# A gated expansion of tokens: the gates move to GpSimd's queue, the first two tokens to the head of SyncE's

## The chip, the cores and the metric

The kernel runs on one core of a Trainium2 chip. The metric is the device time of one execution in microseconds (us); lower is better. Before the change the median of three runs is 92.47 us (92.43 to 92.58). The profile is a separate look at one execution; its span, from the first to the last instruction of the program, is 90.7 us.

## The reference

Each of 8 x 256 = 2048 tokens has a row `x` of 512 values and 8 gate weights. The gates of a token are divided by their sum, and the output holds the token's row eight times, once scaled by each gate:

```python
x:            (8, 256, 512) float32
gate_weights: (8, 256, 8)   float32

gate_weights = gate_weights / (np.sum(gate_weights, axis=-1, keepdims=True) + 1e-8)
output = x[:, :, None, :] * gate_weights[:, :, :, None]      # (8, 256, 8, 512)
```

The input is 4.26 MB and the output 33.55 MB. There is one multiplication for each output value.

## The kernel before

The 2048 tokens are laid over 128 partitions, so that each partition has J = 16 neighbouring tokens. In the text, "token j" is the j-th of each partition: 128 rows of `x`. Everything is kept in SBUF: all gates, all of `x`, and a ring of 10 slots, each with room for one token's eight scaled rows.

The loads are four. The gates (64 KB) and the **head**, tokens 0 and 1 of `x` (512 KB), are moved ahead of the barrier with which the program begins; the **body**, tokens 2 to 12 (2816 KB), and the **tail**, tokens 13 to 15 (768 KB), follow after it on SyncE's queue.

```python
SLOTS = 10
HEAD = 2
TAIL = 13
CHUNKS = ((0, 2, 0), (2, 3, 2), (5, 3, 5), (8, 4, 0), (12, 4, 6))   # first token, tokens, first slot

    first_loads = [
        nc.sync.dma_start(out=g_all, in_=g_v),                                    # L68
        nc.scalar.dma_start(out=x_all[:, 0:HEAD, :], in_=x_v[:, 0:HEAD, :]),      # L69
    ]
    issue_before_entry_barrier(nc, first_loads)
    body_load = nc.sync.dma_start(                                                # L72
        out=x_all[:, HEAD:TAIL, :], in_=x_v[:, HEAD:TAIL, :]
    )
    nc.sync.dma_start(out=x_all[:, TAIL:J, :], in_=x_v[:, TAIL:J, :])             # L75
```

Here `issue_before_entry_barrier` takes the instructions out of their block and puts them at the front of the entry block, ahead of the barrier at which all engines meet.

Then come a small table load on ScalarE (`warm`), the four steps that normalize the gates on VectorE, and the scaling. For tokens 0 and 1 each of the eight experts is an instruction of its own, three on ScalarE and five on VectorE; other tokens are done whole by VectorE or by eight instructions of ScalarE.

```python
    nc.vector.reduce_sum(out=gsum, in_=g_all, axis=mybir.AxisListType.X)          # L80
    nc.vector.tensor_scalar_add(out=gsum, in0=gsum, scalar1=1e-8)                 # L81
    nc.vector.reciprocal(out=gsum, in_=gsum)                                      # L82
    nc.vector.tensor_tensor(out=gn, in0=g_all,                                    # L83
                            in1=gsum.to_broadcast([P, J, E]), op=mult)
    # ... (scale_one: L90 on ScalarE, L92 on VectorE; scale_token: L95 on VectorE)
    for j0, m, s0 in CHUNKS:
        # ... the m tokens of the chunk into slots s0 ...
        store = nc.sync.dma_start(                                                # L120
            out=out_v[:, j0 : j0 + m, :, :], in_=ring[:, s0 : s0 + m, :, :]
        )
        if j0 == 0:
            tc.add_manual_dep(store.ins, body_load.ins.name, ...,
                              reason="no store among the loads")
```

The last lines make the first store (4096 KB) wait for the landing of the body, beside the two tokens that it stores. The other stores are 6144, 6144, 8192 and 8192 KB; all five go through SyncE's queue.

Of the kernel before, what the change touches and what calls it, by code (L numbers as in the profile page):

```python
# [1 line left out]

# [4 lines left out]
# [4 lines that stand above are left out]
CHUNKS = ((0, 2, 0), (2, 3, 2), (5, 3, 5), (8, 4, 0), (12, 4, 6))  # L11


def issue_before_entry_barrier(nc, loads):
    names = [bi.ins.name for bi in loads]

    def move(nc):
        blocks = nc.main_func.blocks
        entry = blocks[0].instructions
        moved = []  # L20
        for block in blocks[1:]:
            for ins in list(block.instructions):
                if ins.name in names:
                    block.instructions.remove(ins)
                    moved.append(ins)
        assert sorted(i.name for i in moved) == sorted(names)
        for ins in moved:
            at = next(k for k, other in enumerate(entry) if other.engine == ins.engine)
            entry.insert(at, ins)

    nc.at_finalize(move)


@with_exitstack
def kernel(
    ctx: ExitStack,
    tc: tile.TileContext,
    x: bass.AP,
    gate_weights: bass.AP,
    out: bass.AP,  # L40
):
    nc = tc.nc
    P = 128

    B, S, D = x.shape
    E = gate_weights.shape[-1]
    J = B * S // P

    fp32 = mybir.dt.float32
    mult = mybir.AluOpType.mult  # L50

    x_v = x.flatten_outer_dims().rearrange("(p j) d -> p j d", p=P)
    g_v = gate_weights.flatten_outer_dims().rearrange("(p j) e -> p j e", p=P)
    out_v = out.rearrange("b s e d -> (b s) e d").rearrange(
        "(p j) e d -> p j e d", p=P
    )

    pool = ctx.enter_context(tc.tile_pool(name="pool", bufs=1))

    g_all = pool.tile([P, J, E], fp32)  # L60
    x_all = pool.tile([P, J, D], fp32)
    ring = pool.tile([P, SLOTS, E, D], fp32)
    gsum = pool.tile([P, J, 1], fp32)
    gn = pool.tile([P, J, E], fp32)
    warm = pool.tile([P, 1], fp32)

    first_loads = [
        nc.sync.dma_start(out=g_all, in_=g_v),  # L68
        nc.scalar.dma_start(out=x_all[:, 0:HEAD, :], in_=x_v[:, 0:HEAD, :]),  # L69
    ]  # L70
    issue_before_entry_barrier(nc, first_loads)
    body_load = nc.sync.dma_start(  # L72
        out=x_all[:, HEAD:TAIL, :], in_=x_v[:, HEAD:TAIL, :]
    )
    nc.sync.dma_start(out=x_all[:, TAIL:J, :], in_=x_v[:, TAIL:J, :])  # L75

    nc.vector.memset(warm, 0.0)  # L77
    nc.scalar.copy(out=warm, in_=warm)  # L78
# [4 lines that stand above are left out]
    nc.vector.tensor_tensor(  # L83
        out=gn, in0=g_all, in1=gsum.to_broadcast([P, J, E]), op=mult
    )

    def scale_one(engine, j, e, slot):
        o_ap, s_ap = ring[:, slot, e, :], gn[:, j, e : e + 1]
        if engine is nc.scalar:
            nc.scalar.mul(out=o_ap, in_=x_all[:, j, :], mul=s_ap)  # L90
        else:
            nc.vector.tensor_scalar_mul(out=o_ap, in0=x_all[:, j, :], scalar1=s_ap)  # L92

    def scale_token(j, slot):
        nc.vector.tensor_tensor(  # L95
            out=ring[:, slot, :, :],
            in0=x_all[:, j : j + 1, :].to_broadcast([P, E, D]),
            in1=gn[:, j, :].unsqueeze(2).to_broadcast([P, E, D]),
            op=mult,
        )  # L100

    for j0, m, s0 in CHUNKS:
        for i in range(m):
            j, slot = j0 + i, s0 + i
            if j < 2:
                for e in range(E):
                    on_act = e < 3
                    scale_one(nc.scalar if on_act else nc.vector, j, e, slot)
            elif j == 2:
                for e in range(E):  # L110
                    scale_one(nc.scalar, j, e, slot)
            elif j == 3:
                for e in range(E):
                    scale_one(nc.scalar if e < 2 else nc.vector, j, e, slot)
            elif i == 0:
                for e in range(E):
                    scale_one(nc.scalar, j, e, slot)
            else:
                scale_token(j, slot)
# [4 lines that stand above are left out]
            tc.add_manual_dep(  # L124
                store.ins,
                body_load.ins.name,
                mybir.DependencyInfo(
                    mybir.DependencyClass.Sync, mybir.DependencyReason.DATA
                ),
                reason="no store among the loads",  # L130
            )


# [1 line left out]
_INS = ['x', 'gate_weights']  # L135
_OUTS = [((8, 256, 8, 512), 'float32')]


# [23 lines left out]
```

## Time and profile before

| | |
|---|---|
| time, median of 3 | 92.47 us |
| span of the profile | 90.7 us |
| VectorE busy | 46.7 us |
| ScalarE busy | 26.4 us |
| bytes read, written | 4.26 MB, 33.55 MB |
| first store issued | 10.60 us |
| chunk of the first store computed | 7.96 us |

Each number of a time is counted from the first instruction of the span. A line of the profile names the line of the kernel (L68), the engine (DVE is VectorE, ACT is ScalarE, POOL is GpSimd, SP is SyncE; with a q it is the engine's sequencer, which issues transfers), the operation, output and inputs by the program's names, and how many instructions are meant. "Idle before, releaser" is the time for which the engine stood idle ahead of it, and what ended that. The list of DMA issues has the time from the issue to the landing, that is to the moment from which the waiting engines may go on. In the row of 40 slices a digit is the busy share of a fortieth of the span in tenths; transfers in long packets are counted at the slice of the packet's start or end, so neighbouring windows can swing above and below what was moved.

### The profile page before, as it was taken

To read this page: it belongs to the slowest core of one execution; us is meant where nothing else is said; L and a number is where in the kernel's file an instruction comes from. 1 tells how busy PE (TensorE), PEld (TensorE's weight loads), DVE (VectorE), ACT (ScalarE), POOL (GpSimd) and SP (SyncE) were. 2 spreads that over 40 slices of the span, in tenths; PEclk is the share of its full clock that TensorE was granted. 3 is DMA by queue.
4 is the path that set the end of the run, shared out by engine and by line. 5 is a ranking of instruction groups with operands and counts; after the bars stand their busy time and mean duration, and the time that the engine had idled before them with its cause. 6 is when DMAs were issued, how large, how long until landed. Compare 5 with 4: busy or idle time off the path is not lost.

```text
span 90.7 us, 140 instructions
## 1 busy us (share of the span) xinstructions
DVE 46.7 (52%) x30; ACT 26.4 (29%) x42; POOL 0.2 (0%) x4
## 2 busy tenths in 40 slices
DVE  0795399999999999999990495000000000000000
ACT  5393399997990000000000497000000000000000
POOL 0000000000000000000000000000000000000000
DMA  4998999999898889888988999999999982999990
GB/s 110 468 467 378 383 536 463 463 390 419 347 694 347 347 347 694 347 347 347 694 347 347 463 463 463 463 463 463 463 463 463 463 347 116 463 463 463 463 463 0
DMA packets 1296, 37.81 MB, mean 417 GB/s; under 512 B 144, under 2 KB 272, under 8 KB 528
## 3 DMA queue, kind: packets, MB, share of 16 engines
q1 hardware_dynamic: 1152, 37.29, 95.5%
q10 hardware_dynamic: 144, 0.52, 1.6%
HBM read 4.26 MB, written 33.55 MB: 417 GB/s over the span
## 4 chain that ended last, share of the span: by engine, by line
DMA 38%; DVE 17%; ACT 5%; ACTq 1%; issue 0%; SPq 0%
DMA out_dram<-ring 28%; DVE ring L95 14%; DMA x_all<-in_x_dram 11%; ACT ring L90 5%; DVE ring L92 3%; ACTq L157 1%; ACTq L90 0%; SPq L120 0%
## 5 line engine op out<-in xcount | busy, mean ns | idle before, releaser
L95 DVE TENSOR_TENSOR ring<-x_all,gn 128x4096 f32<-128x4096 f32 x9 | 39.2, 4420 | 3.5 <-DMA out_dram<-ring 3.5
L90 ACT ACTIVATE ring<-x_all,gn 128x512 f32<-128x512 f32 x40 | 24.9, 708 | 28.8 <-DMA out_dram<-ring 24.5
L92 DVE TENSOR_SCALAR ring<-x_all,gn 128x512 f32<-128x512 f32 x16 | 6.5, 482 | 2.8 <-DMA x_all<-in_x_dram 2.8
L78 ACT ACT_TABLE_LOAD x1 | 1.3, 1283 | 0.9 <-PEq L146 0.9
L80 DVE TENSOR_REDUCE gsum<-g_all 128x16 f32<-128x128 f32 x1 | 0.3, 286 | 1.6 <-DMA g_all<-in_gate_weights_dram 1.6
L77 DVE MEMSET warm<- 128x1 f32 x1 | 0.1, 59 | 1.0 <-PEq L146 1.0
L83 DVE TENSOR_TENSOR gn<-g_all,gsum 128x128 f32<-128x128 f32 x1 | 0.3, 291 | 0.0
L82 DVE RECIPROCAL gsum<-gsum 128x16 f32<-128x16 f32 x1 | 0.3, 252 | 0.0
L78 ACT COPY warm<-warm 128x1 f32<-128x1 f32 x1 | 0.2, 191 | 0.0
L81 DVE TENSOR_SCALAR gsum<-gsum 128x16 f32<-128x16 f32 x1 | 0.2, 176 | 0.0
L146 POOL MEMSET const-bfloat16-1.0<- 128x1 bf16 x1 | 0.1, 102 | 0.0
L146 POOL MEMSET const-uint8-127<- 128x1 uint8 x1 | 0.1, 102 | 0.0
L146 POOL MEMSET const-float32-0.0<- 128x1 f32 x1 | 0.1, 99 | 0.2 <-issue 0.2
L146 POOL MEMSET const-float32-1.0<- 128x1 f32 x1 | 0.1, 99 | 0.0
## 6 DMA issues: line engine op xcount, KB each, us to landing
out_dram<-ring SPq DMA_DIRECT2D x2, 6144.0 KB, 22.1
out_dram<-ring SPq DMA_DIRECT2D x1, 4096.0 KB, 11.5
x_all<-in_x_dram SPq DMA_DIRECT2D x1, 2816.0 KB, 9.6
x_all<-in_x_dram SPq DMA_DIRECT2D x1, 768.0 KB, 11.1
x_all<-in_x_dram ACTq DMA_DIRECT2D x1, 512.0 KB, 3.7
g_all<-in_gate_weights_dram SPq DMA_DIRECT2D x1, 64.0 KB, 2.6
out_dram<-ring SPq DMA_DIRECT2D x2, 28.1
```

The lines of the kernel that those rows point to most:

```text
L77: nc.vector.memset(warm, 0.0)
L78: nc.scalar.copy(out=warm, in_=warm)
L80: nc.vector.reduce_sum(out=gsum, in_=g_all, axis=mybir.AxisListType.X)
L81: nc.vector.tensor_scalar_add(out=gsum, in0=gsum, scalar1=1e-8)
L82: nc.vector.reciprocal(out=gsum, in_=gsum)
L83: nc.vector.tensor_tensor(out=gn, in0=g_all, in1=gsum.to_broadcast([P, J, E]), op=mult)
L90: nc.scalar.mul(out=o_ap, in_=x_all[:, j, :], mul=s_ap)
L92: nc.vector.tensor_scalar_mul(out=o_ap, in0=x_all[:, j, :], scalar1=s_ap)
L95: nc.vector.tensor_tensor(out=ring[:, slot, :, :], in0=x_all[:, j : j + 1, :].to_broadcast([P, E, D]), in1=gn[:, j, :].unsqueeze(2).to_bro ...
L146: nc = _bacc.Bacc("TRN2", target_bir_lowering=False, num_devices=1)
L157: with _tile.TileContext(nc) as tc:
```

## The change

The head of `x` takes the place of the gates at the front of SyncE's queue, still ahead of the barrier. The gates are loaded through GpSimd's queue, after the barrier. ScalarE issues no load any more. The purpose is to let the larger transfer start first and to spread the issuing over queues.

```diff
     first_loads = [
-        nc.sync.dma_start(out=g_all, in_=g_v),
-        nc.scalar.dma_start(out=x_all[:, 0:HEAD, :], in_=x_v[:, 0:HEAD, :]),
+        nc.sync.dma_start(out=x_all[:, 0:HEAD, :], in_=x_v[:, 0:HEAD, :]),
     ]
     issue_before_entry_barrier(nc, first_loads)
+    nc.gpsimd.dma_start(out=g_all, in_=g_v)
     body_load = nc.sync.dma_start(
         out=x_all[:, HEAD:TAIL, :], in_=x_v[:, HEAD:TAIL, :]
     )
```

The order of instructions on VectorE and ScalarE, apart from the issue that ScalarE loses, stays what it was.

## The prediction

> **What bounds the kernel now.** I read the page first, then the chain of waits, then the timeline of the first 11 us, because the change touches only the loads. On the page, the transfers are busy nearly all the time and no engine is:
>
> ```profile
> span 90.7 us, 140 instructions
> DVE 46.7 (52%) x30; ACT 26.4 (29%) x42; POOL 0.2 (0%) x4
> DMA  4998999999898889888988999999999982999990
> HBM read 4.26 MB, written 33.55 MB: 417 GB/s over the span
> ```
>
> The two compute engines are busy for 52% and 29% of the span, while the DMA row stands at 8 or 9 tenths from the second slice almost to the end. So the kernel is a stream of 37.8 MB (4.26 read, 33.55 written), and it ends when the stream ends. A change of the loads can count in two ways: it moves the start of the stream, or it tears a hole into it. The place where a hole can open is the seam between the last load and the first store. The timeline, cut to its first 11 us, shows the seam; the columns are start, length, engine, line and operation, and the bracket is the idle time before it and what ended that.
>
> ```profile
> 0.00 0.38 SPq L68 DMA_DIRECT2D g_all<-in_gate_weights_dram  x1
> 0.12 0.36 ACTq L69 DMA_DIRECT2D x_all<-in_x_dram  x1
> ...
> 0.91 0.33 SPq L72 DMA_DIRECT2D x_all<-in_x_dram  x1
> 1.30 0.42 SPq L75 DMA_DIRECT2D x_all<-in_x_dram  x1
> 2.61 0.29 DVE L80 TENSOR_REDUCE gsum<-g_all 128x16 f32<-128x128 f32 x1 [1.57 <-DMA g_all<-in_gate_weights_dram]
> ...
> 3.91 4.05 DVE L92 TENSOR_SCALAR ring<-x_all,gn 128x512 f32<-128x512 f32 x10 [0.19 <-DMA x_all<-in_x_dram]
> 10.53 11.14 ACT L90 ACTIVATE ring<-x_all,gn 128x512 f32<-128x512 f32 x18 [2.86 <-DMA x_all<-in_x_dram]
> ```
>
> The gates are on chip at 2.61, four small VectorE steps normalize them, and the first two tokens are computed from 3.91 to 7.96 (3.91 + 4.05) on VectorE; ScalarE's share ends a little earlier. Then both engines sit idle until the eleven tokens of the body land at 10.5. The SyncE queue's own waits name the same event for the first store:
>
> ```profile
> SPq L157 <- DMA out_dram<-ring: 33.1, 1, 33.1
> SPq L120 <- DMA x_all<-in_x_dram: 8.8, 1, 8.8
> ```
>
> It waits 8.8 us for the body load, and issues the store at 10.60. The first line is the end: after the last issue the queue waits 33.1 us for stores. The chunk was finished at 7.96, so the gates have **a slack of 10.51 − 7.96 = 2.55 us**: landing up to about 5.2 us they would cost nothing. The list of DMA issues gives the sizes and the time from issue to landing:
>
> ```profile
> x_all<-in_x_dram SPq DMA_DIRECT2D x1, 2816.0 KB, 9.6
> x_all<-in_x_dram SPq DMA_DIRECT2D x1, 768.0 KB, 11.1
> x_all<-in_x_dram ACTq DMA_DIRECT2D x1, 512.0 KB, 3.7
> g_all<-in_gate_weights_dram SPq DMA_DIRECT2D x1, 64.0 KB, 2.6
> ```
>
> Landings are therefore: gates 2.6, head 0.12 + 3.7 = 3.8, body 0.91 + 9.6 = 10.5, tail 1.30 + 11.1 = 12.4. The tail keeps the transfers busy while the first store gets under way. From 12.4 on there are only stores, and 33.55 MB from 12.4 to the last landing near 89.6 is 434 GB/s.
>
> One more thing is to be read from these landings, and my prediction hangs on it. The body was issued at 0.91 and the head, on another queue, was still coming in until 3.8. If the two had shared the DMA engines packet by packet, the body would have had a good part of its bytes by then. Yet from 3.8 to 10.5 it took 6.7 us for 2.88 MB, which is 430 GB/s, the full rate. So **practically all of the body came after the head**: a transfer that arrives later, on another queue, stood behind what the DMA engines had already taken up.
>
> **What the Trainium skill says.** "DMA: Bandwidth & Descriptors", section "Queues, rings and completion order": each DMA engine goes round between the queues at the granularity of packets, and drains a whole packet, typically 9 to 17 descriptors, before it switches. A load over 128 partitions is 8 rows and a completion per engine, so a packet of nine could be an engine's whole share of a load. The landings of head and body agree with that, although they don't prove it. The same page, section "SWDGE vs HWDGE vs iDMA", says that GpSimd's descriptors are made by software and put in a ring, with packets of preferably 4096 B at most; under "Specifications" it gives about 1 us to the first byte on this path against about 0.6 us for the SyncE and ScalarE queues. Here a view by windows shows no traffic before 1.0 us for the issue at 0.0, so 1.0 us is what the trace has for SyncE; no load of GpSimd is in this trace.
>
> **The change part by part.**
>
> (a) The head goes to SyncE ahead of the barrier and ScalarE's issue of 0.36 us disappears. The head starts at 0.0 instead of 0.12 and has no 64 KB of gates ahead of it (65.5 KB / 430 GB/s = 0.15 us). It lands some 0.3 us earlier, at about 3.5. Nobody gains directly: the head is used only once the gates are normalized.
>
> (b) The body and the tail are issued where they were, at about 0.9 and 1.3. The body loses the 64 KB ahead of it and lands 0.1 to 0.3 us earlier, near 10.3. The number of bytes is the same, so the stream as a whole gains nothing but a slightly fuller first microsecond: 0.2 us at most.
>
> (c) The gates leave SyncE at 0.0 and are issued by GpSimd after the barrier at about 0.9, with a slower start. I put their descriptors with the DMA engines at 0.9 + 1.0 + 0.4 to 1.0 = 2.3 to 2.9 us (1.0 measured on SyncE, 0.4 from the difference of the two figures of the skill, the rest allowance; an estimate). By then the body, ready at 0.9 + 1.0 = 1.9, is already queued on each of the 16 engines. The gates need every one of them, for 128 rows of 512 B lie on all.
>
> (d) From the landing of the gates to the end of the first chunk: 7.96 − 2.61 = 5.35, of which 0.19 was a wait for the head that is now over, so 5.2 us. If the body is drained first, the gates land with it, 10.3 + 0.15 for their own bytes = 10.5. The first chunk is then done at 10.5 + 5.2 = 15.7, and the store goes out there and not at 10.60: **5.1 us later**. The tail covers the transfers until 12.4; then they stand idle. In the old kernel the first store also stood behind the tail (11.5 us to land 4.19 MB, of which 9.7 are bytes at 434 GB/s); without it the store would land in about 11.1, which returns 0.3 us. Net +4.8 us. Later compute has 3.3 us and more in hand (the fourth store is issued at 47.76 and its predecessor lands at 51.1) and is moved along with the stores, so nothing of it is regained: 92.47 + 4.8 = **97.3 us**.
>
> **The rivals.** *The gates slip in.* If the engines switch after one row of 22.5 KB (2816 KB over 128 rows is 22.5 KB each, eight rows per engine; one row at 430/16 = 27 GB/s per engine is 0.83 us) and the eight gate rows of an engine, 4096 B, count as one packet, the gates wait for one or two body rows: 2.6 + 0.8 to 1.7 + 0.2 for the bytes + 0.4 to complete = 4.0 to 4.9. That is within the slack of 2.55 us; the first store still waits for the body and only (b) is left: 92.2 to 92.6 us. For it speaks that GpSimd's queue is one of its own; against it that the body didn't slip in beside the head. *One gate row per body row*: eight turns of 0.83 us, landing at about 2.6 + 6.7 + 0.4 = 9.7, and a time of 96.5, hardly to be told from my main case. *The gates land behind the tail as well*, at about 12.4: chunk done at 17.6, store 7.0 later, some 99 us. For it speaks that the tail is issued at 1.3, perhaps before the gate descriptors are complete. *An engine becomes the bound*: no, both compute engines have tens of microseconds to spare.
>
> **Range and chances.** The outcome has two heaps, not one. Behind the body (or one row for one) I give 0.55, slipping in 0.37, behind the tail too 0.08. Two per cent is 1.85 us, so everything but the second heap is slower by more than that. Within the first heap the uncertain terms (when the body lands, how soon the completion follows) are about 0.7 us. A range for 8 in 10 must reach from the good heap to the bad one: 92.2 to 98.4. Faster by over 2% is nearly excluded, as the bytes stay the same.
>
> **What would show it.** In the changed profile: VectorE's reduction of the gates starts at about 10.5 with a long wait for the gates' load (the main case), or at 4 to 5 us (they slipped in). The issue of the first store stands at about 15.7, and SyncE waits there for VectorE and no longer for the body; the DMA row has a hole of some 4 us around 13 to 17 us. The load by GpSimd shows about 9.5 us from issue to landing. The head lands near 3.5, the body near 10.3. I am wrong if DMA engines serve a small packet of another queue between two rows of the body, or if GpSimd's descriptors reach the engines before the body's do.

## The result and the profile after

The changed kernel takes 95.12 us (median of four runs, 94.94 to 95.26) beside 92.45 us for the kernel before: a ratio of 1.0273, 95% interval 1.0236 to 1.0310. That is 2.67 us more. The time lies inside the predicted range, but in the gap between its two heaps, and 2.2 us below the point that was given.

The timeline of the changed kernel, cut to the lines that answer to those of before (start, length, engine, line and operation; in brackets the idle time and what ended it):

```profile
0.00 0.38 SPq L68 DMA_DIRECT2D x_all<-in_x_dram  x1
...
0.79 0.33 SPq L72 DMA_DIRECT2D x_all<-in_x_dram  x1
...
1.28 0.66 POOL L71 DMA_DIRECT2D g_all<-in_gate_weights_dram  x1 [0.84 <-PEq L157]
...
8.27 0.29 DVE L80 TENSOR_REDUCE gsum<-g_all 128x16 f32<-128x128 f32 x1 [7.35 <-DMA g_all<-in_gate_weights_dram]
...
9.41 6.43 DVE L92 TENSOR_SCALAR ring<-x_all,gn 128x512 f32<-128x512 f32 x16
13.54 15.71 SPq L120 DMA_DIRECT2D out_dram<-ring  x3
```

The reduction of the gates starts at 8.27 where it started at 2.61. The first store goes out at 13.54, not at 10.60. The group of sixteen products has no idle time in it: when the first two tokens are done the body has long been there. What SyncE waited for before that store has changed its name, in the waits of its queue:

```profile
SPq L120 <- DVE ring L92: 11.9, 1, 11.9
```

and the chain of work that ended last, in order of time, begins with the gates' load instead of the body's:

```profile
1.28 6.97 DMA g_all<-in_gate_weights_dram
...
9.41 4.06 DVE ring L92 x10
...
13.54 11.15 DMA out_dram<-ring
```

The price is paid in the transfers. The tail lands at 1.17 + 11.7 = 12.9 us, and a view by windows shows what happens around that time (length; busy time of VectorE, ScalarE and GpSimd with instructions; clock; DMA share; GB/s):

```profile
12.60:14.30 1.70, 1.70 (x6) 1.70 (x3) 0.00 (x0) 1.00 0.00 0
```

For 1.7 us no packet starts on any engine, while both compute engines are fully busy. For a single DMA engine the hole is longer. By the records of the packets the engines ended with the loads at 11.5 to 12.5 us and began with the store at 14.4 to 14.5, so that an engine stood idle for 2.6 us in the mean. In the kernel before, the store's first packet followed the last one of the loads by 0.01 us in the mean: the store stood ready behind the tail. The list of DMA issues closes the sum:

```profile
out_dram<-ring SPq DMA_DIRECT2D x1, 4096.0 KB, 11.2
...
g_all<-in_gate_weights_dram POOLq DMA_DIRECT2D x1, 64.0 KB, 7.0
```

The store is issued 13.54 − 10.60 = 2.94 us later and lands in 11.2 us instead of 11.5, so some 2.6 us are lost at its landing (24.7 against 22.1), as much as the hole is long. Nothing later gives any of it back, and the whole kernel is 2.67 us slower.

What is not explained by this is why a load of 64 KB took 7.0 us. One line of the DMA queues of the changed kernel is of use (packets, MB, share):

```profile
q0 software_dynamic: 32, 0.07, 0.2%
```

There are 32 packets for 16 DMA engines, two each: one of 64 KB / 16 = 4096 B with an engine's eight rows of gates, and one of 4 B, the completion; the last of the sixteen completions starts at 7.90 us, 0.35 us before the landing. The records of the packets give their times. They carry no engine; an engine's sequence is put together from records of which each starts where another ended. One such sequence, in ns from the start of the span, reads:

```
3077 body row 22528 B | 3910 body row | 4743 body row | 5576 body row |
6409 gates 4096 B (159 ns) | 6564 body row (836 ns) | 7397 gates' completion | 7403 body row | ...
```

The gates come in after four rows of the body (three on one engine, four on all others, at 5.7 to 6.6 us), and then the completion waits for one body row more. The engines take turns, but the turn comes late.

### The profile page after: what moved, and what is told of

The parts are those of the page before. It is cut to its first block, busy times and chain, and to the rows that moved or that the text cites. A ratio compares the mean times of both kernels' runs of the same rounds, so it can differ in the third digit from the quotient of the medians.

```text
span 93.4 us, 140 instructions
## 1 busy us (share of the span) xinstructions
DVE 46.6 (50%) x30; ACT 26.3 (28%) x42; POOL 0.9 (1%) x5
## 3 DMA queue, kind: packets, MB, share of 16 engines
q1 hardware_dynamic: 1152, 37.75, 94.6%
## 4 chain that ended last, share of the span: by engine, by line
DMA 46%; ACT 9%; DVE 5%; issue 1%; ACTq 1%; POOLq 0%; SPq 0%
DMA out_dram<-ring 39%; ACT ring L90 9%; DMA g_all<-in_gate_weights_dram 7%; DVE ring L92 4%; ACTq L157 1%; DVE gn L83 0%; DVE gsum L80 0%; DVE gsum L82 0%; DVE gsum L81 0%; ACTq L90 0%; POOLq L157 0%; SPq L120 0%; POOLq L146 0%
## 5 line engine op out<-in xcount | busy, mean ns | idle before, releaser
L71 POOL DMA_DIRECT2D g_all<-in_gate_weights_dram x1 | 0.7, 661 | 0.8 <-PEq L157 0.8
## 6 DMA issues: line engine op xcount, KB each, us to landing
out_dram<-ring SPq DMA_DIRECT2D x1, 4096.0 KB, 11.2
x_all<-in_x_dram SPq DMA_DIRECT2D x1, 768.0 KB, 11.7
```

Source lines behind the costliest of these rows:

```text
L71: nc.gpsimd.dma_start(out=g_all, in_=g_v)
```

## The experiments

Two theories stood at the start. **Turns**: the gates' descriptors are with the engines early, and wait for rows of the body that are already taken up. **Slow issue**: GpSimd's way of issuing is itself late by several microseconds. The edits below are made to the changed kernel unless it is said otherwise. Lines of a kernel are counted anew in each, so L numbers differ. All kernels compute the whole reference. The last section of this part has all results in a table.

**1. The gates with nothing but the head beside them** (`body_behind_gates`).

```diff
+for load in (body_load, tail_load):
+    tc.add_manual_dep(load.ins, gates_load.ins.name, ..., reason="no body or tail beside the gates")
```

> The body and the tail are issued only when the gates have landed, so that GpSimd's load meets nothing but the head on the DMA engines. Theory of turns (the gates' descriptors are ready early, at about 2.5 to 3 us, and wait for rows of the body that the engines have taken up): the gates land at 3.3 to 4.2 us, not at 8.2. Theory of the slow issue (GpSimd's software needs until about 5 to 6 us whatever else is under way): they land at 7 to 8 us. In both the time is above that of the kernel before, as the loads now have a hole; with turns about 94 us, with the slow issue 97 to 98.

From the list of DMA issues:

```profile
g_all<-in_gate_weights_dram POOLq DMA_DIRECT2D x1, 64.0 KB, 2.7
```

Issued at 1.26, landed at 4.0: with the head alone beside it, GpSimd's load is about as quick as SyncE's in the kernel before (2.6 us), and its rows move at 3.1 to 3.5 us, not at 5.7 to 6.6. The slow issue falls. The time is 95.40 us, 1.4 us more than the 94 expected with turns, as the loads now have a hole of their own (body issued at 4.03, first store at 13.31).

**2. Shorter rows of the body.** If the gates wait for rows, shorter rows must help. First the body in two loads, with rows of 12 and 10 KB:

```diff
-body_load = nc.sync.dma_start(out=x_all[:, HEAD:TAIL, :], in_=x_v[:, HEAD:TAIL, :])
+nc.sync.dma_start(out=x_all[:, HEAD:8, :], in_=x_v[:, HEAD:8, :])
+body_load = nc.sync.dma_start(out=x_all[:, 8:TAIL, :], in_=x_v[:, 8:TAIL, :])
```

> The body is cut into two loads, tokens 2 to 7 and 8 to 12, so that its rows are 12 and 10 KB instead of 22.5. Theory of turns counted in rows (about four rows taken up, then the gates, one row more, then the completion): rows last 0.46 us instead of 0.83, and the gates land at 5.6 to 6.2; the time falls to 92.6 to 93.3. Turns counted in bytes (the engines have taken up some 90 KB each): the data comes in as in the changed kernel and only the completion's turn is shorter, landing 7.7 to 8.0, time 94.6 to 94.9. Slow issue: 7.7 to 8.2 as well, time 94.6 to 95.1.

Then rows of one token, by a tile of its own for the body in which the tokens lie 16 elements apart:

```diff
+x_body = pool.tile([P, TAIL - HEAD, D + 16], fp32)
-    out=x_all[:, HEAD:TAIL, :], in_=x_v[:, HEAD:TAIL, :]
+    out=x_body[:, :, 0:D], in_=x_v[:, HEAD:TAIL, :]
```

> The body lands in a tile whose tokens are padded apart, so that each row is one token, 2 KB, 88 rows per engine, at the same bytes and the same one issue. Theory of turns counted in rows: five rows of 0.08 us are nothing, the gates land at 3.3 to 4.2, the store waits for the body again, time 92.2 to 92.9 if the short rows keep the rate. Counted in bytes: landing 6.5 to 7.2, time 93.4 to 94. Slow issue: the same 6.5 to 7.5.

The gates' landing, from the same list, of half_rows and then of small_rows:

```profile
g_all<-in_gate_weights_dram POOLq DMA_DIRECT2D x1, 64.0 KB, 7.0
```

```profile
g_all<-in_gate_weights_dram POOLq DMA_DIRECT2D x1, 64.0 KB, 5.7
```

With rows eleven times shorter the gates gained 1.3 us (7.0, store at 12.29, 93.93 us), not the 4 to 5 that counting in rows asked for. So the wait isn't counted in rows. By the packet records an engine's gates follow 36 to 38 rows of 2 KB in small_rows (27 to 43 at the extremes), six or seven rows of 12 KB in half_rows and four of 22.5 KB in the changed kernel: mostly 70 to 90 KB each time, or about 3 us. The shorter row speeds up the turn of the completion.

In the trace of half_rows the gates landed at 8.28 and the first store went out at 13.55, as in the changed kernel. But the traced execution took 95.27 us and the other three 94.43 to 94.67, and in it one engine's gates came in only at 7.3 us, where the others had theirs at 5.9 to 6.9. The completion's turn was shorter there too (one row of 0.46 us, not 0.83). The median of 94.59 us is what was expected of a count in bytes, 94.6 to 94.9; the landing at 7.7 to 8.0 that belonged to it was not seen in this trace.

**3. The gates by ScalarE after the barrier** (`gates_act_after_barrier`).

```diff
-nc.gpsimd.dma_start(out=g_all, in_=g_v)
+nc.scalar.dma_start(out=g_all, in_=g_v)
```

> The gates are issued by ScalarE after the barrier instead of by GpSimd. If GpSimd's way of making descriptors is what makes them late, they now land at 3 to 4 us and the time is 92.2 to 92.7. If the place behind the barrier is what counts (the body is queued first) and the engines take turns row by row, the gates' eight rows per engine, each a turn of its own, need as many rows of the body: landing 9 to 10.7, slower than the changed kernel, 96 to 97.5. If an engine gives all eight in one turn, landing 7 to 8.3 and about 95.

From its DMA queues and issues:

```profile
q10 hardware_dynamic: 144, 0.07, 0.2%
...
g_all<-in_gate_weights_dram ACTq DMA_DIRECT2D x1, 64.0 KB, 9.9
```

Here the same 64 KB are 144 packets, 128 rows and 16 completions, where GpSimd's were 32. The records of one engine are a strict alternation: 2930 body row, 3763 gate row (27 ns), 3786 body row, 4619 gate row, 4643 body row, and so on to the last gate row at 9758 and the gates' completion at 9788. One short row for one long row; the gates land at 10.7, with the body, and the time is 97.66 us. So taking GpSimd out does not cure it, and the changed kernel, with eight rows in one packet, is 2.5 us faster than this. Issued in the same moment as the body (0.79 us), the first gate row waited for one row of the body only: there was no long queue ahead of it yet.

**4. The queue ahead, without GpSimd** (`small_rows_act_late`). Do the 3 us of experiment 2 belong to the engines or to GpSimd's path when the engines are busy? Body rows of 2 KB as in small_rows, and ScalarE issues the gates as late as GpSimd's descriptors were ready:

```diff
+warm_copy = nc.scalar.copy(out=warm, in_=warm)
+gates_load = nc.scalar.dma_start(out=g_all, in_=g_v)
+tc.add_manual_dep(gates_load.ins, warm_copy.ins.name, ..., reason="gates issued late")
```

> The body's rows are 2 KB as in small_rows, and the gates are issued by ScalarE after its table load, at about 2.3 us, so that their descriptors should be with the DMA engines at about 3.3, as late as those of GpSimd were in body_behind_gates (landing at 4.0 there). The question is where the 3 us go that GpSimd's gates lose beside the body, and that stayed with rows of 22.5, 12 and 2 KB. Theory of a long queue of bytes (each engine has taken up some 80 KB and serves it first, whoever comes later): the gates land at 6.9 to 7.8 as well. Theory of GpSimd's path (its descriptors themselves come late when the engines are busy): ScalarE's gates only take turns with rows of 0.08 us and land at 4.2 to 5.2; the first store then waits for the body again and the time is 92.3 to 93.0.

```profile
2.29 0.36 ACTq L79 DMA_DIRECT2D g_all<-in_gate_weights_dram  x1
...
7.58 0.29 DVE L89 TENSOR_REDUCE gsum<-g_all 128x16 f32<-128x128 f32 x1 [6.67 <-DMA g_all<-in_gate_weights_dram]
```

The gates land at 7.58, 5.3 us after the issue; in the kernel before 2.6 us did. The first gate rows move at 6.0 to 6.3 us, when the body has been coming in for 3 us, on all engines. The queue ahead is there for ScalarE's load as well: **issued 0.5 us (GpSimd) or 1.5 us (ScalarE) after the body, the gates wait some 3 us behind it, whoever issues them**. At 27 GB/s per engine (a row of 22.5 KB in 0.83 us) that is about 80 KB, an estimate. Whether the engines hold a number of bytes or a span of time these runs don't tell, as all bodies came in at nearly the same rate.

**5. GpSimd ahead of the barrier** (`pool_before_barrier`).

```diff
     first_loads = [
         nc.sync.dma_start(out=x_all[:, 0:HEAD, :], in_=x_v[:, 0:HEAD, :]),
+        nc.gpsimd.dma_start(out=g_all, in_=g_v),        # placed behind GpSimd's four memsets
     ]
-nc.gpsimd.dma_start(out=g_all, in_=g_v)
```

> The changed kernel with GpSimd's issue moved ahead of the barrier, behind GpSimd's four small memsets: at about 0.5 instead of 1.3 us, the same queue. If coming ahead of the body is all that counts, the gates' descriptors are there at about 2.2, while the head is still coming in, and land at 3.3 to 4.5; the time is 92.3 to 93 (the barrier may open up to 0.7 us later, as GpSimd comes to it later). If GpSimd's path is slow whenever the engines are busy, they land some 7 us after the issue, at 7.3 to 7.7: 94.0 to 94.8.

From the waits of SyncE's queue:

```profile
SPq L152 <- PEq L152: 3.8, 1, 3.8
```

The barrier held SyncE for 3.8 us. It opened at 4.4, shortly after the gates' landing at 0.83 + 3.3 = 4.1, and only then could the body be issued. The time is 95.46 us. The landing is early only because nothing was beside it, so the run does not bear on the two theories; it shows another cost. That GpSimd comes to the barrier only when its load is complete fits the times, but was not tried apart.

**6. Each part alone, and the place.** Only the gates' part (`gates_part_alone`: the head back on ScalarE ahead of the barrier):

```diff
-    nc.sync.dma_start(out=x_all[:, 0:HEAD, :], in_=x_v[:, 0:HEAD, :]),
+    nc.scalar.dma_start(out=x_all[:, 0:HEAD, :], in_=x_v[:, 0:HEAD, :]),
```

> Only the gates' part of the change: the head stays on ScalarE ahead of the barrier, the gates go through GpSimd after it. If the gates are the whole cost, the landing is 7.8 to 8.5 and the time that of the changed kernel, 94.8 to 95.6. If the head in front on SyncE's queue is part of it (because body and tail follow it on one queue), the gates land earlier and the time is below 94.3.

The gates land at 8.1 and the time is 95.24 us, a ratio of 1.0274 as for the whole change: the gates' part is the whole loss. The counterpart (`swap_queues`) keeps the head in front on SyncE and issues the gates by ScalarE, both ahead of the barrier:

```diff
 first_loads = [
     nc.sync.dma_start(out=x_all[:, 0:HEAD, :], in_=x_v[:, 0:HEAD, :]),
+    nc.scalar.dma_start(out=g_all, in_=g_v),
 ]
-nc.gpsimd.dma_start(out=g_all, in_=g_v)
```

> The kernel before with its two early loads exchanged: the head on SyncE, the gates on ScalarE, both ahead of the barrier. The gates' descriptors are on the engines before the body's, and a turn is at most a head row of 0.16 us: landing 2.7 to 3.6, within the slack; the store waits for the body. Both theories: the time is that of the kernel before within 0.4 us, 92.1 to 92.8. If it is clearly above, then what the head does at the front of SyncE's queue costs something in itself.

The time is 92.53 us, the ratio 0.9987 (0.9965 to 1.0009): that of the kernel before. Its profile is of one of the two executions in twenty-two that took much longer, 95.0 us. In it the gates landed at 0.12 + 3.7 = 3.8 us, and by the packet records one engine began with the body only at 5.8 us, the other fifteen at 3.0 to 3.5; the body landed at 0.92 + 12.3 = 13.2. Experiment 8 comes back to this.

**7. A shorter path behind late gates** (`split_first_chunk`).

```diff
-CHUNKS = ((0, 2, 0), (2, 3, 2), ...
+CHUNKS = ((0, 1, 0), (1, 1, 1), (2, 3, 2), ...
```

> The changed kernel with its first store cut in two, one token each, so that the path from the gates to the first store has five VectorE products and not ten, some 2.0 us less. The gates land at 8.2 as before. If the loss is just the hole in the transfers between the tail and the first store, as the two traces say, the store goes out at about 11.5, its first bytes follow the tail at once, and nearly all of the loss is gone although the gates are as late as ever: 92.5 to 93.2. If late gates cost in another way as well (the later products, the ring's slots), the time stays above 94.

```profile
11.81 2.31 SPq L120 DMA_DIRECT2D out_dram<-ring  x2
```

The gates are late as ever, at 8.5, yet the first store is out at 11.81 and the time is 93.72 us, a ratio of 1.0111: more than half of the loss is gone with nothing changed in the loads. That late gates cost through the first store's issue is shown by this. (What the split does to the kernel before was not tried.) The size was missed: the gates landed 0.3 us later than assumed, and the store's first packet starts 0.85 us after its issue, at 12.65, when the loads are already through. The remaining 1.15 us answers to a store that is still 11.81 − 10.60 = 1.2 us late.

The hole at the seam follows the loss from run to run. In the mean of the engines it is 2.6 us in the changed kernel, 2.3 in gates_part_alone, 1.4 in small_rows_act_late, 0.9 in small_rows and 0.8 here; lost were 2.7, 2.6, 1.9, 1.0 and 1.15 us.

**8. Behind the barrier, but ahead of the body** (`gates_sync_ahead_of_body`, and its neighbour `head_part_alone` with both loads on SyncE ahead of the barrier).

```diff
-nc.gpsimd.dma_start(out=g_all, in_=g_v)
+nc.sync.dma_start(out=g_all, in_=g_v)          # gates_sync_ahead_of_body
```

> The gates are issued after the barrier, as in the change, but by SyncE and just ahead of the body. If it is the place behind the body that makes them late, they now come in behind the head alone, landing 3.2 to 4.0; the store waits for the body: 92.3 to 92.9 (the body is issued 0.4 us later, which the head still covers). If being behind the barrier costs in itself, 93.5 and more.

> Both early loads on SyncE ahead of the barrier, the head first, the gates second; ScalarE and GpSimd issue none. It is the head's part of the change without the late gates. Landing of the gates 2.8 to 3.8, inside the slack; time 92.2 to 92.8, that of the kernel before.

In both the gates land at 3.85, about as expected: for their landing the barrier does not matter, the place before the body does. And in both the time is some 2.2% above, 94.71 and 94.65 us, which I had not expected. The store waits for the body again, and it is the body that lands late. In head_part_alone it is issued at 1.28 and takes 11.3 us where it took 9.6:

```profile
x_all<-in_x_dram SPq DMA_DIRECT2D x1, 2816.0 KB, 11.3
```

The windows from 5.5 to 7 us, of the kernel before and then of head_part_alone, show transfers at about half the rate:

```profile
5.50:7.00 1.50, 1.50 (x5) 1.50 (x4) 0.00 (x0) 1.00 1.12 481
```

```profile
5.50:7.00 1.50, 1.50 (x5) 1.50 (x4) 0.00 (x0) 1.00 0.79 255
```

By the packet records seven of the sixteen engines in head_part_alone, and five in gates_sync_ahead_of_body, begin with the body only at 4.6 to 5.4 us, two microseconds after the others. The last run put body and tail on ScalarE's queue (`head_part_body_act`, the edit is to head_part_alone):

```diff
-body_load = nc.sync.dma_start(
+body_load = nc.scalar.dma_start(
-nc.sync.dma_start(out=x_all[:, TAIL:J, :], in_=x_v[:, TAIL:J, :])
+nc.scalar.dma_start(out=x_all[:, TAIL:J, :], in_=x_v[:, TAIL:J, :])
```

> head_part_alone with body and tail issued by ScalarE after the barrier instead of SyncE. There the gates landed in time, at 3.9, and yet the body landed 2.1 us late, at 12.6, which neither theory had foreseen. If that is because the body stands on the same queue behind head and gates, it now lands at 10.6 to 11.2 and the time is 92.3 to 93.2. If it comes from the gates' short rows reaching the engines just ahead of the body, whatever the queue, the body lands at 12.2 to 12.8 again: 94.2 to 95.

```profile
x_all<-in_x_dram ACTq DMA_DIRECT2D x1, 2816.0 KB, 11.4
```

The body lands at 12.7 again (five engines late), and the time is 94.36 us. So sharing a queue with the head and the gates is not the cause. What these three have in common is that the gates' short rows come in between the head and the body, at 2.7 to 3.5 us; in the kernel before they are in at 1.0 to 2.2. That alone does not settle it: in the traced execution of swap_queues the short rows come in at 2.5 to 3.4, among the head's last rows and behind them, and one engine started late, yet its usual time is that of the kernel before. Why some engines start late stays open.

**All results**, landings and first store from the profiles, in us:

| kernel | gates landed | first store | time | ratio to before (95%) |
|---|---|---|---|---|
| before | 2.6 | 10.60 | 92.45 | |
| changed | 8.25 | 13.54 | 95.12 | 1.0273 (1.0236 to 1.0310) |
| body_behind_gates | 4.0 | 13.31 | 95.40 | 1.0262 (1.0211 to 1.0313) |
| half_rows | 8.3 | 13.55 | 94.59 | 1.0193 (1.0136 to 1.0250) |
| small_rows | 7.0 | 12.29 | 93.93 | 1.0111 (1.0067 to 1.0154) |
| gates_act_after_barrier | 10.7 | 16.03 | 97.66 | 1.0507 (1.0453 to 1.0560) |
| small_rows_act_late | 7.6 | 12.85 | 94.49 | 1.0185 (1.0141 to 1.0230) |
| pool_before_barrier | 4.1 | 13.75 | 95.46 | 1.0284 (1.0230 to 1.0338) |
| gates_part_alone | 8.1 | 13.38 | 95.24 | 1.0274 (1.0223 to 1.0326) |
| swap_queues | 3.8 (in 95.0 us) | 13.27 (in 95.0 us) | 92.53 | 0.9987 (0.9965 to 1.0009) |
| split_first_chunk | 8.5 | 11.81 | 93.72 | 1.0111 (1.0071 to 1.0151) |
| gates_sync_ahead_of_body | 3.85 | 12.72 | 94.71 | 1.0219 (1.0179 to 1.0259) |
| head_part_alone | 3.85 | 12.65 | 94.65 | 1.0226 (1.0177 to 1.0276) |
| head_part_body_act | 3.9 | 12.77 | 94.36 | 1.0177 (1.0128 to 1.0226) |

Times of different rows were taken beside different runs of the kernel before (92.45 to 92.95 us), so the ratio is the column to compare. For swap_queues landing and store are those of the execution of 95.0 us. No version is faster than the kernel before; swap_queues equals it.

## Why the prediction was right and where it was wrong

**Right: what bounds, and how the loss arises.** The stream of transfers is the bound, the seam behind the tail is where it tears, and the slack is what it was taken for. The path of part (d) was put at 5.2 us; the trace has 13.54 − 8.25 = 5.29, and the other runs in which the store waited for the gates have the same 5.3. The return of 0.3 us by a store with no tail ahead of it was exact (11.2 against 11.5 us). Part (a), nothing gained by the head in front, is borne out by swap_queues. The head landed at 3.6 (predicted 3.5).

**Luck: the range.** It held because it was stretched from the good heap to the bad one. The measured 95.12 us lies between the 92.6 of the gates that slip in and the 96.5 of one gate row per body row, where no case of the prediction lay.

**Wrong: the step "if the body is drained first, the gates land with it", in part (d).** It put the landing at 10.5; it was 8.25. The 2.25 us between them are nearly the whole error of the point: a store at 13.54 instead of 15.7, and 95.1 us instead of 97.3. The body was not drained first: a gates packet came in between two rows of it, which the prediction had named as a sign of being wrong. The reading behind that step was that the body had come wholly after the head, hence a late load stands behind all that is ahead of it. The observation was sound, the conclusion too wide. An engine's share of the head is 32 KB, less than the roughly 80 KB that experiment 4 finds taken up ahead; a head of that size cannot tell a queue of 80 KB from a queue without end.

**The rival had the mechanism, with a mis-sized term.** "The gates slip in" assumed turns of one packet and one packet for an engine's eight gate rows, and both are so: 32 packets in the changed kernel, and the single rows of ScalarE's load alternate one to one with the body's. The Trainium skill's statement that engines go round packet by packet ("DMA: Bandwidth & Descriptors", section "Queues, rings and completion order") agrees with these traces; its 9 to 17 descriptors for a typical packet do not describe these loads by ScalarE and SyncE, where each row was a turn of its own (144 packets for 128 rows and 16 completions). The wrong term is the wait, "one or two body rows", 0.8 to 1.7 us. In the packets it was four rows before the data (3.3 us) and one more before the completion (0.83 us), 4.2 us. Split by the runs, the landing is the issue at 1.28, plus 2.7 for the load without the body (body_behind_gates), plus 3.0 that rows of 2 KB leave (small_rows), plus 1.3 that the long rows add, the completion's turn of 0.83 among them: 8.3. The last two terms are differences of landings, so the sum holds by construction. The third rival, row for row, came true in experiment 3, with ScalarE as the issuer, within 1.2 us of its 96.5.

**Also off, with little effect.** GpSimd's issue starts at 1.28 and not at 0.9, and takes 0.66 us. The allowance for a slower first byte on its path was of no consequence: alone it landed 2.7 us after its issue, SyncE's 2.6. The body landed at 10.8 and not near 10.3, but no one was waiting for it. The hole was 2.6 us long in the mean of the engines and not some 4, as the store went out 2.2 us earlier than predicted.

## What to carry to other kernels

A small load on which the first computation depends should be with the DMA engines before a large load is. Another queue did not overtake here: behind a body already issued it cost some 3 us and then a turn for each packet. But where it stands among the early loads needs a run too: at the very front, or from ScalarE beside the head, it cost nothing, while between head and body on SyncE's queue the gates were in time and the body came 2 us late. To judge such a change, take the slack of the small load from the trace, and compare it with the time of what is already taken up and not only with the load's latency alone. Where the load must be late, shorten what lies between it and the first store: one token instead of two returned more than half of the loss.

## What the runs showed of the hardware that was not expected

- The eight 512 B rows of an engine travelled as one packet of 4096 B when GpSimd issued them (32 packets in all) and as eight when ScalarE did (144); beside the same body that was 7.0 us against 9.9 us from issue to landing.
- The completion of GpSimd's load is a packet of its own and waits for a turn: with its data in at 6.4, an engine wrote it at 7.4, one row of the body later.
- A load by GpSimd ahead of the entry barrier held the barrier until 4.4 us, 0.3 us after it had landed.
- With the gates' short rows between head and body, five to seven of sixteen engines started on the body some 2 us late, whether the body was on SyncE's queue or on ScalarE's; the cause is not known.
